# Expert layer on one Trainium2 core: 76 instead of 72 of 128 expert columns by fetched rows

## The chip, the cores and the metric

One core of a Trainium2 chip. The metric is device time in microseconds for one execution of the whole program (both transformer blocks); less is better. Engines are named as in the profile: PE (matrix engine), PEld (its weight loads), DVE (vector), ACT (scalar), POOL (GpSimd), SP (the queue that issues plain DMAs). POOL issues the indirect DMAs.

## What is computed

256 tokens of width 2048 pass a first block (two attentions, then an expert layer) and a second block (gated linear attention, pooling, an MLP of width 8192). The change touches the expert layer alone. Cut to what matters:

```python
q = (xt @ w_q).reshape(T, 8, 2, 128)                  # T = 256 tokens, 8 heads
s = einsum('thpd,hpnd->thpn', q, sub_keys)            # 128 keys in each half
# top 16 of each half, then top 16 of their 256 sums, per head
idx = i_first * 128 + i_second                        # one of 16384 experts
g = softmax(top_s)                                    # 8 x 16 = 128 experts a token
a = einsum('td,ted->te', xt, expert_u[idx])
y = einsum('te,ted->td', g * gelu(a), expert_v[idx])
```

So each token uses 128 of 16384 experts. With the experts as a grid of 128 x 128, the second half of the index is called the column here.

## The kernel before

Nearly all products are made to full precision by splitting both sides into a high and a low part (`hi_lo`, L196: ACT makes the high part, DVE the low one) and adding three matmuls (`mm3`, L217). `stream` (L204) loads a 512 KB piece of a weight into a buffer `r` and splits it into `h` and `l`; three buffers of each are in turn. PE's work is almost all on line L192, the helper `mm`.

The expert layer (`experts`, L903) computes a = x·u for **all** 16384 experts, one grid column a step (i = 0 to 127, 48 matmuls of 256 columns and two 512 KB loads of `u` a step). What follows depends on the column:

- **Columns below PICKED** (72): the activations go, four columns at a time (`lot`, 512 KB), to a table `picked` in DRAM. Of these columns only the experts that tokens have chosen are used: `pack` (L1113) sorts each group of 32 tokens' choices into 21 packs (PACKS) of 128 slots. The choices fill a group's packs from the first on, so that the last of the 21 are partly or wholly empty. For each of the 8 x 21 = 168 packs `fetch_act` (L1152) gathers the 128 activations and `fetch_row` (L1156) gathers up to 128 rows of 8 KB from `v_rows`; an empty slot points beyond the table and moves nothing. `multiply` (L1163) adds a pack's rows, weighted, into the group's output with four matmuls of 512 columns, which the profile counts as eight.
- **Columns from PICKED on** (GRID = 56): the activations stay in SBUF in `gridt` (56 columns x 256 tokens), multiplied by the gates, which `build` (L1080) and `apply` (L1094) spread over the grid with one-hot matmuls, four tokens at a time (64 times). Then `dense_rows` (L862) multiplies the whole grid with these columns of `v`: two halves of the output (d = 0, 1), one step a column, each step a 512 KB load of `v`, its split, the split of the column's weights, and 12 matmuls of 512 columns.

The steps run in this order: x·u for i = 0 to 127 (the u stage), then 2 x 56 steps of `dense_rows` (the v stage). Packing and building lie between the steps of the u stage, from i = 23 and i = 57 on. The picks (`picks`, L1177) are woven in by `unit` (L1228): each half step of the u stage from i = PICKED + LEADP = 75 on, and each v step up to the 40th of the second half (LASTY), adds PACE = 0.84 to a credit; at 3 (LOT) three packs are multiplied at once, back to back. After a pack's `multiply`, POOL issues the fetch of the pack six later (FETCH = 6 buffers) and the gather of activations twelve later. At i = PICKED - 1 the last `lot` is stored, twelve gathers of activations are issued, and DVE's `weigh` (L1160), which multiplies gates and activations four packs at a time, waits for them. When the grid's steps reach LASTY, the picks are done (16 steps remain); their sums are added to the result from DRAM (`add_y`, L1302). A branch behind it (`beyond`) works off what does not fit into 21 packs of a group; it runs only if a group has more than 21 x 128 = 2688 choices.

At the start of the v stage SP also loads 2 MB of the saved residual (`h2t<-h_keep`). `gridt` serves as scratch for the choosing of experts before the grid is filled; `carve` cuts tables from its end, one of them `pk`, a constant of 260 floats a partition.

Of the kernel before, what the change touches and what calls it, by code (L numbers as in the profile page):

```python
# [10 lines left out]
F32 = mybir.dt.float32  # L11
# [15 lines left out]
T = 256  # L27
NM = 16
TM = T + NM
PICKED = 72  # L30
GRID = 128 - PICKED
GROUP = 32
PACKS = 21
# [58 lines left out]
def _layout(a):  # L92
# [34 lines left out]
    v = a["peer_v"][0].reshape(128, 128, D)  # L127
    L["v"] = v[:, PICKED:].reshape(128, GRID, 2, 1024).transpose(2, 1, 0, 3).reshape(2 * GRID, 128, 1024)
    L["v_rows"] = v[:, :PICKED].reshape(128 * PICKED, D)

# [175 lines left out]
def bc(ap, shape):  # L306
    return ap.to_broadcast(shape)
# [531 lines left out]
FIRST, RATE = 57, 4  # L839
FETCH = 6  # L840
AHEAD, SOON = 12, 4
LASTY = 40
LOT = 3
LEADP, PACE = 3, 0.84


def topk16(S, jobs):
# [14 lines left out]
def dense_rows(S, wp, src, nk, get, evac, last=0, last_pool=None):  # L862

    mm = S.mm
    for d in range(2):
        accs = [[S.bank() for _ in range(2)] for _ in range(2)]

        def products(i, t, w, v, cols=(0, 1)):  # L870
            ts = slice(t * 128, t * 128 + 128)
            for a, b, first, end in ((w[0], v[0], True, False), (w[0], v[1], False, False), (w[1], v[0], False, True)):
                for c in cols:
                    mm(accs[t][c], a[:, ts], b[:, c], start=first and i == 0, stop=end and i == nk - 1)

        kept = []
        for i in range(nk):
            hold = d == 1 and i >= nk - last
            v = S.stream(src[d * nk + i], 2, 512, last_pool if hold else None)
            pool = last_pool if hold else wp  # L880
            w = [pool.tile([128, T], F32R, tag=f"w{x}", name=S.name("w")) for x in "hl"]
            S.hi_lo(get(i), *w)
            if hold:
                kept.append((i, w, v))
                products(i, 0, w, v)
            else:
                for t in range(2):
                    products(i, t, w, v)
            yield d, i
        yield d, nk  # L890
        for t in range(2):
            for c in range(2):
                if t == 1:
                    for i, w, v in kept:
                        products(i, 1, w, v, (c,))
                evac(d, t, c, accs[t][c])
# [6 lines left out]
def experts(S, I, x2, r2, started, keep, bst, grid, alloc_xn, close_x2, close_xn, late, picked, y_rows):  # L903
# [12 lines left out]
    def carve(*shape, dt=F32):  # L916
        n = int(np.prod(shape))
        end[0] -= n
        t = scratch[:, end[0]:end[0] + n].bitcast(dt)
        if len(shape) > 1:  # L920
            t = t.rearrange("p (a n) -> p a n", a=shape[0])
        if len(shape) > 2:
            t = t.rearrange("p a (b n) -> p a b n", b=shape[1])
        return t
# [13 lines left out]
    sc_ = carve(2, 16, 128)  # L938
    keysT = carve(16, 128)
    bcr = carve(T)  # L940
    pk = carve(260)
    spare = [carve(T) for _ in range(4)]
    S.load(keysT, I["keysT"])
    S.load(pk, I["c_pick"])

    def renorm(k):
# [34 lines left out]
    ow = ob.enter_context(tc.tile_pool(name="oneh", bufs=2))  # L981
# [15 lines left out]
    def choose():  # L997
        iota16 = S.iota[:, 0:16]
        for t in range(2):
# [57 lines left out]
            n = es[:, 0:1]  # L1057
            po.tensor_scalar(x, ii[:, 1], PICKED - 0.5, None, ALU.is_lt)
            ve.tensor_reduce(n, x, axis=AX, op=ALU.add)
            ve.tensor_scalar(y, S.ones, n, None, ALU.mult)  # L1060
            po.tensor_scalar(x, slots[:, 1, ts], PICKED - 0.5, None, ALU.is_lt)
            yield
# [17 lines left out]
    def build(t0):  # L1080

        iota = bc(S.iota[:, None, :], [128, 4, 128])
        of = lambda s, n: bc(slots[:, s, t0:t0 + 4][:, :, None], [128, 4, n])
        oh = ow.tile([128, 4, 128], F32R, tag="oh", name=S.name("oh"))
        ec = ow.tile([128, 4, GRID], F32, tag="ec", name=S.name("ec"))
        gv = ow.tile([128, 4, 2, GRID], F32R, tag="gv", bufs=1, name=S.name("gv"))
        ve.tensor_tensor(oh, iota, of(0, 128), op=ALU.is_equal)
        ve.tensor_tensor(ec, iota[:, :, PICKED:], of(1, GRID), op=ALU.is_equal)
        ve.tensor_tensor(gv[:, :, 1], ec, of(3, GRID), op=ALU.mult)
        for tt in range(4):  # L1090
            act.activation(gv[:, tt, 0], ec[:, tt], AF.Copy, scale=slots[:, 2, t0 + tt:t0 + tt + 1])
        made[t0] = oh, gv, ec
# [109 lines left out]
    def beyond():  # L1202

        more = 4096 // 128 - PACKS
        for g in range(8):
            for _ in pack(g, PACKS, more, 0):
                pass
            out = S.bank()
            for n in range(more):
                fetch_act(n)  # L1210
                fetch_row(n, fetched[n % FETCH])
                weigh(n)
                multiply(out, n, fetched[n % FETCH], n == 0, n == more - 1)
            stage = rw.tile([128, 512], F32, tag="stage", name=S.name("stage"))
            for c in range(4):
                S.load(stage[GROUP * c:GROUP * c + GROUP], y_rows[GROUP * g:GROUP * g + GROUP, 512 * c:512 * c + 512])
            ve.tensor_tensor(stage, stage, out, op=ALU.add)
            for c in range(4):
                S.load(y_rows[GROUP * g:GROUP * g + GROUP, 512 * c:512 * c + 512], stage[GROUP * c:GROUP * c + GROUP])
# [8 lines left out]
    def unit():  # L1228

        nonlocal credit  # L1230
        credit += PACE
        if credit >= LOT:
            for _ in range(LOT):
                next(side, None)
            credit -= LOT

    for i in range(128):
# [29 lines left out]
        if i == FIRST - 2:  # L1267
            for _ in bg:
                pass
            S.token = None  # L1270
            for f in fetched + [got]:
                po.memset(f, 0.0)
            for n in range(FETCH):
                fetch_row(n, fetched[n])
            build(0)
            ahead = 4
# [25 lines left out]
    def add_y(h, t, c):  # L1302
        y = rw.tile([128, 4, T], F32, tag="lot", name=S.name("y")).rearrange("p a b -> p (a b)")
        cs = slice(1024 * c, 1024 * c + 1024)
        po.dma_start(y, y_rows[t * 128:t * 128 + 128, cs])
        ve.tensor_tensor(h[:, t, cs], h[:, t, cs], y, op=ALU.add)
# [5 lines left out]
    for d, i in dense_rows(S, wp, I["v"], GRID, lambda i: grid[:, i], evac):  # L1312
        if d == 0 and i < GRID or d == 1 and i < LASTY:
            unit()
        if d == 1 and i == LASTY:
            for _ in side:
                pass
            S.pe_token = None
        if d == 1 and i == LASTY:
            n = nc.values_load(most_i[0:1, 0:1], min_val=0, max_val=4096)  # L1320
            with tc.If(n > 128 * PACKS):
                beyond()
        if d == 1 and LASTY < i <= LASTY + 2:
            add_y(h, i - LASTY - 1, 0)
        step(d, i)
# [356 lines left out]
    mst.close()  # L1682


FEAT = 47


class Plan:
# [20 lines left out]

    def alloc_x2(self):  # L1710
        self.bst = ExitStack()
        self.grid = self.bst.enter_context(self.S.tc.tile_pool(name="grid", bufs=1)).tile([128, GRID, T], F32, name="gridt")
        return self.parts("x2", side="left", first=192)

    def late(self):
# [11 lines left out]
        def step(d, i):  # L1727
            if d == 0:
                return
            if i == 0:  # L1730
# [4 lines left out]
                self.close("meta")  # L1735
            if i in (FEAT, FEAT + 6):
                self.features((i - FEAT) // 6)
            if i == GRID:
# [19 lines left out]
def program(tc, I, out):  # L1758
    with ExitStack() as st:
        S = Core(tc, st)  # L1760
        dram = st.enter_context(tc.tile_pool(name="dram", bufs=1, space=DRAM))
        keep = dram.tile([2, 128, D], F32, name="h_keep")
        base = S.const.tile([128, 384], F32, name="base")
        S.ident, S.iota, S.ones = base[:, 0:128], base[:, 128:256], base[:, 256:384]
        S.gains = S.const.tile([128, 98], F32, name="gains")
        S.load(S.gains, I["gains"])
        S.load_base = lambda: S.load(base, I["c_base"])
        warm = S.const.tile([128, 1], F32, name="warm")
        S.nc.vector.memset(warm, 0.0)
        S.nc.scalar.copy(warm, warm)  # L1770
        R = Plan(S, I)
        x2, r2, started = front(S, I, keep, R.alloc_x2, lambda j, x2: query(S, I, j, x2))
        picked = dram.tile([128, PICKED, T], F32, name="picked")
        y_rows = dram.tile([T, D], F32, name="y_rows")
        h = experts(S, I, x2, r2, started, keep, R.bst, R.grid, lambda: R.parts("xn"), lambda: R.close("x2"), lambda: R.close("xn"), R.late,
                    picked, y_rows)
        R.rest()
        back(S, I, h, R.u, R.started, R.ssn, lambda: R.close("ub", "ua"), out)
        R.close("h2")
# [11 lines left out]
```

## Time and profile before

| what | value |
|---|---|
| median of 3 runs (lowest to highest) | 2735.54 us (2732.2 to 2744.61) |
| the profiled execution | 2743.11 us |
| its span (first to last instruction) | 2741.0 us |
| PE busy | 2668.8 us, 97% |
| DVE, ACT, POOL busy | 62%, 49%, 25% |
| mean granted PE clock | 0.992 |
| u stage, first 72 steps | 425 to 855 us |
| u stage, 56 steps with grid and picks | 855 to 1292 us |
| v stage, steps with picks | 1292 to 1640 us |

"DMA share" is the busy share of the core's 16 DMA engines, added up over packets, so it can show slightly over 1. Busy time of PE is made of modelled ends: matmuls overlap, and the distance between starts says more than the duration of one. An idle time stands in brackets before what ended it.

### The profile page before, as it was taken

The page shows a single profiled execution, that of the slowest core. Times are in us where ns is not written, and L with a number is a line of the kernel's source. Part 1 is how long each engine was busy: PE and PEld are TensorE (multiplying, and loading weights), DVE is VectorE, ACT ScalarE, POOL GpSimd, SP SyncE. Part 2 cuts the span into 40 slices and gives each one's busy share as a digit, 9 for nine tenths or more (in the row PEclk, how much of TensorE's full clock was granted, in tenths as well). Part 3 has the DMA queues.
Part 4 walks back from the last instruction along what each step waited for, and adds up shares of the span by engine and source line. Part 5 has one row for each costly group of instructions (what it writes and reads, how often), then busy time and mean ns, then how long its engine had stood idle before and what let it go on. Part 6 is the DMA issues. An engine that isn't in the chain of part 4 may idle for free. (4 is left out here: it accounts for less than half of the span.)

```text
span 2741.0 us, 48520 instructions
## 1 busy us (share of the span) xinstructions
PE 2668.8 (97%) x18644; PEld 2328.6 (85%) x18644; DVE 1710.7 (62%) x3048; ACT 1336.7 (49%) x2330; POOL 683.8 (25%) x764
## 2 busy tenths in 40 slices
PE   7999999999999999999999997999999999999998
PEld 6977899999998888887666666998889999988886
DVE  5867787768866676774455455645554444566665
ACT  5655544434354444443444444534455555555554
POOL 1300003244613656665564520102000000000000
PEclk9999999999999999999999998999999999999999
DMA  6533756676665888899999985454666666666665
GB/s 214 156 121 107 224 174 195 207 249 222 189 196 162 323 329 328 319 365 354 373 391 374 363 308 187 135 152 137 187 186 195 196 193 193 194 195 194 189 196 162
DMA packets 161727, 625.89 MB, mean 228 GB/s; under 512 B 25849, under 2 KB 26873, under 8 KB 141321
## 3 DMA queue, kind: packets, MB, share of 16 engines
q1 hardware_dynamic: 131344, 462.77, 52.2%
q0 software_dynamic: 30144, 159.95, 14.9%
q8 instruction: 148, 2.42, 0.3%
q14 instruction: 91, 0.75, 0.1%
HBM read 625.33 MB, written 15.73 MB: 234 GB/s over the span
## 5 line engine op out<-in xcount | busy, mean ns | idle before, releaser
L198 DVE TENSOR_TENSOR l<-r,h 128x1024 fp32r<-128x1024 f32 (+3 forms) x838 | 1027.4, 1228 | 618.1 <-ACT h L197 592.5
L197 ACT ACTIVATE h<-r 128x1024 fp32r<-128x1024 f32 (+3 forms) x838 | 878.2, 1049 | 922.8 <-PE bank L192 656.0
L192 PE MATMUL bank<-xnh,l 128*128 128x256 f32 x2048 | 575.1, 281 | 11.7 <-DVE l L198 6.2
L192 PE MATMUL bank<-xnh,h 128*128 128x256 f32 x2048 | 582.4, 284 | 3.5 <-ACT h L197 2.7
L192 PE MATMUL bank<-xnl,h 128*128 128x256 f32 x2048 | 573.9, 280 | 0.6 <-issue 0.5
L192 PE MATMUL bank<-h,w 128*128 128x512 f32 x1920 | 523.5, 391 | 3.6 <-ACT w L197 2.0
L192 PEld LDWEIGHTS bank<-h,w 128*128 128x128 f32 x1920 | 357.6, 188 | 102.1 <-issue 18.4
L192 PEld LDWEIGHTS bank<-xnh,h 128*128 128x128 f32 x2048 | 391.7, 191 | 15.9 <-issue 7.1
L192 PEld LDWEIGHTS bank<-xnh,l 128*128 128x128 f32 x2048 | 388.0, 189 | 14.6 <-DVE l L198 7.2
L192 PEld LDWEIGHTS bank<-xnl,h 128*128 128x128 f32 x2048 | 388.4, 190 | 0.9 <-issue 0.8
L192 PE MATMUL bank<-l,w 128*128 128x512 f32 x960 | 297.4, 390 | 0.9 <-DVE l L198 0.9
L192 PE MATMUL bank<-zh,h 128*128 128x256 f32 x1024 | 283.0, 276 | 0.0
L192 PE MATMUL bank<-zl,h 128*128 128x256 f32 x1024 | 282.9, 276 | 0.0
L192 PE MATMUL bank<-zh,l 128*128 128x256 f32 x1024 | 282.9, 276 | 0.0
L1148 POOL DMA_INDIRECT fetched<-v_rows,at_row x168 | 205.5, 1223 | 230.4 <-PE bank L192 197.2
L192 PEld LDWEIGHTS bank<-l,w 128*128 128x128 f32 x960 | 179.9, 188 | 39.8 <-DVE l L198 2.2
L1148 POOL DMA_INDIRECT got<-picked,at_act x168 | 193.7, 1153 | 56.4 <-issue 49.7
L192 PEld LDWEIGHTS bank<-zh,l 128*128 128x128 f32 x1024 | 192.3, 188 | 0.0
L192 PEld LDWEIGHTS bank<-zh,h 128*128 128x128 f32 x1024 | 192.2, 188 | 0.0
L192 PEld LDWEIGHTS bank<-zl,h 128*128 128x128 f32 x1024 | 192.2, 188 | 0.0
L1124 POOL TENSOR_TENSOR what<-mine,facts 128x126 bf16<-128x126 f32 x256 | 140.2, 577 | 173.7 <-PE bank L1127 156.8
L1668 POOL TENSOR_TENSOR h2t<-h2t,fw 128x512 f32<-128x512 f32 x4 | 6.4, 1642 | 638.7 <-ACT jk L1666 638.7
(452 smaller groups left out, 3921.8 us busy)
## 6 DMA issues: line engine op xcount, KB each, us to landing
r<-u SPq DMA_DIRECT2D x256, 512.0 KB
r<-w SPq DMA_DIRECT2D x256, 512.0 KB
r<-v SPq DMA_DIRECT2D x112, 512.0 KB
r<-w_out SPq DMA_DIRECT2D x64, 512.0 KB
r<-wq SPq DMA_DIRECT2D x32, 512.0 KB
r<-w_in_c SPq DMA_DIRECT2D x24, 384.0 KB
picked<-lot SPq DMA_DIRECT2D x18, 512.0 KB
r<-w_v SPq DMA_DIRECT2D x16, 512.0 KB
```

What stands on the lines that cost most here:

```text
L192: i = self.nc.tensor.matmul(*args, **kw)
L197: self.nc.scalar.activation(hi, src, AF.Copy)
L198: self.order(self.nc.vector.tensor_tensor(lo, src, hi.bitcast(F32), op=ALU.subtract))
L1124: po.tensor_tensor(what[:, tt], bc(mine[:, tt][:, None, :], [128, 6, n]), bc(facts[:, :, t0 + tt][:, :, None], [128, 6, n]), op=ALU.mult)
L1148: i = po.indirect_dma_start(*args, **kw)
L1668: po.tensor_tensor(hs, hs, fw[:, cs_], op=ALU.mult)
```

## The change

PICKED goes from 72 to 76, so GRID from 56 to 52. LASTY and FEAT (a step of the v stage at which the next block's first work begins) are now written from GRID, and lie as far from the end of the v stage as before (16 and 9 steps). PACE goes from 0.84 to 0.91. The scratch tables no longer fit into the smaller grid, so `pk` gets a place of its own beside it. PACKS stays at 21. The layout of `v` and `v_rows` follows PICKED.

```diff
-PICKED = 72
+PICKED = 76
 GRID = 128 - PICKED
 GROUP = 32
 PACKS = 21
...
-LASTY = 40
+LASTY = GRID - 16
 LOT = 3
-LEADP, PACE = 3, 0.84
+LEADP, PACE = 3, 0.91
...
     bcr = carve(T)
-    pk = carve(260)
     spare = [carve(T) for _ in range(4)]
     S.load(keysT, I["keysT"])
+    pk = S.pk[:, :260]
     S.load(pk, I["c_pick"])
...
-        ec = ow.tile([128, 4, GRID], F32, tag="ec", name=S.name("ec"))
+        ec = ow.tile([128, 4, 56], F32, tag="ec", name=S.name("ec"))[:, :, :GRID]
...
-FEAT = 47
+FEAT = GRID - 9
...
-        self.grid = self.bst.enter_context(self.S.tc.tile_pool(name="grid", bufs=1)).tile([128, GRID, T], F32, name="gridt")
+        p = self.bst.enter_context(self.S.tc.tile_pool(name="grid", bufs=1))
+        self.grid = p.tile([128, GRID, T], F32, name="gridt")
+        self.S.pk = p.tile([128, 320], F32, name="pk")
```

Where instructions move, at two places. **DVE in the v stage**, from the last pack of a lot of three (L1166 makes a pack's weights `w` from slot and gate) to the first of the next lot; a row `w<-gridt` is one step of the grid. Before:

```order
L1166 TENSOR_SCALAR w_17582<-base,tok,gate 128x32
L198 TENSOR_TENSOR w_17418<-gridt,w_17417 128x256
L198 TENSOR_TENSOR l_17435<-r_17433,h_17434 128x1024
L1161 TENSOR_TENSOR gate<-gate,got 128x4
L198 TENSOR_TENSOR w_17440<-gridt,w_17439 128x256
L198 TENSOR_TENSOR l_17493<-r_17491,h_17492 128x1024
L198 TENSOR_TENSOR w_17498<-gridt,w_17497 128x256
L198 TENSOR_TENSOR l_17515<-r_17513,h_17514 128x1024
L198 TENSOR_TENSOR w_17520<-gridt,w_17519 128x256
L1166 TENSOR_SCALAR w_17682<-base,tok,gate 128x32
```

and now:

```order
L1166 TENSOR_SCALAR w_17620<-base,tok,gate 128x32
L198 TENSOR_TENSOR w_17455<-gridt,w_17454 128x256
L198 TENSOR_TENSOR l_17509<-r_17507,h_17508 128x1024
L198 TENSOR_TENSOR w_17514<-gridt,w_17513 128x256
L198 TENSOR_TENSOR l_17531<-r_17529,h_17530 128x1024
L1161 TENSOR_TENSOR gate<-gate,got 128x4
L198 TENSOR_TENSOR w_17536<-gridt,w_17535 128x256
L1166 TENSOR_SCALAR w_17698<-base,tok,gate 128x32
```

Between two lots stand four steps in the first piece and three in the second. Both kinds occur in both kernels: in PE's order of the v stage 27 lots stand there before and now, 15 of them with four and 11 with three steps ahead before, 8 with four and 18 with three now (the first lot has fewer).

**DVE where the picks start**, from the last one-hot table before the first `weigh` (L1161) on. Before:

```order
L1087 TENSOR_TENSOR oh_10485<-base,slots 128x512
L1161 TENSOR_TENSOR gate<-gate,got 128x4
L1260 TENSOR_TENSOR gridt<-gridt,gelu_10383 128x64
L198 TENSOR_TENSOR l_10508<-r_10506,h_10507 128x1024
L1106 TENSOR_TENSOR ec_10305<-ec_10305,bank_10396 128x4
```

and now:

```order
L1087 TENSOR_TENSOR oh_10830<-base,slots 128x512
L1260 TENSOR_TENSOR gridt<-gridt,gelu_10729 128x80
L1161 TENSOR_TENSOR gate<-gate,got 128x4
L198 TENSOR_TENSOR l_10853<-r_10851,h_10852 128x1024
L1106 TENSOR_TENSOR ec_10651<-ec_10651,bank_10742 128x4
```

The first `weigh` stands four steps later in the u stage (the grid's first column then has 80 gated tokens in place of 64), and the low part `l` of a piece of `u` still stands behind it.

## Rows read from the trace of the kernel before

**Rows 1.** The page's part 2, DMA in 40 slices of the span.

```profile
DMA  6533756676665888899999985454666666666665
```

**Rows 2.** Busy time by stretch: stretch, length, each engine's busy time, clock, DMA.

```profile
core 0: us, PE busy (x) PEld busy (x) DVE busy (x) ACT busy (x) POOL busy (x), PEclk, DMA share, GB/s
...
855.00:895.00 40.00, 33.32 (x264) 31.55 (x267) 24.03 (x58) 16.88 (x44) 17.25 (x20) 0.91 0.41 130
895.00:1292.00 397.00, 392.00 (x3398) 327.65 (x3391) 272.09 (x585) 186.54 (x467) 252.26 (x253) 1.00 0.90 337
1292.00:1340.00 48.00, 45.04 (x233) 28.86 (x235) 20.73 (x38) 17.48 (x27) 23.09 (x21) 1.00 1.02 401
1340.00:1600.00 260.00, 259.16 (x1370) 176.14 (x1363) 133.35 (x225) 106.90 (x150) 145.67 (x122) 1.00 0.97 374
1380.00:1420.00 40.00, 40.00 (x212) 27.22 (x209) 20.10 (x36) 15.81 (x23) 22.75 (x20) 1.00 1.02 410
```

**Rows 3.** Groups of instructions by line, whole span: busy, mean ns, idle before.

```profile
L198 DVE TENSOR_TENSOR l<-r,h 128x1024 fp32r<-128x1024 f32 (+3 forms) x838 | 1027.4, 1228 | 618.1 <-ACT h L197 592.5 <-issue 23.5
L192 PE MATMUL bank<-fetched,w 128*32 128x512 f32 x1344 | 155.8, 596 | 0.0
L198 DVE TENSOR_TENSOR w<-gridt,w 128x256 fp32r<-128x256 f32 x112 | 47.2, 422 | 40.3 <-PE bank L192 34.1 <-issue 5.6 <-ACT w L197 0.2
L1099 PE MATMUL bank<-gv,oh 128*128 128x112 f32 x256 | 39.2, 274 | 3.5 <-DVE ec L1106 2.5 <-DVE tmp L1134 0.4 <-DVE gv L1089 0.3
```

**Rows 4.** PE's timeline in the v stage, lots of three packs: start, duration.

```profile
1297.88 2.78 PE L192 MATMUL bank<-fetched,w 128*32 128x512 f32 x24
...
1309.73 2.78 PE L192 MATMUL bank<-fetched,w 128*32 128x512 f32 x24
...
1327.14 2.78 PE L192 MATMUL bank<-fetched,w 128*32 128x512 f32 x24
...
1338.81 2.78 PE L192 MATMUL bank<-fetched,w 128*32 128x512 f32 x24
...
1366.46 2.78 PE L192 MATMUL bank<-fetched,w 128*32 128x512 f32 x24
...
1377.58 2.78 PE L192 MATMUL bank<-fetched,w 128*32 128x512 f32 x24
...
1391.41 2.78 PE L192 MATMUL bank<-fetched,w 128*32 128x512 f32 x24
...
1491.29 2.78 PE L192 MATMUL bank<-fetched,w 128*32 128x512 f32 x24
...
1506.35 2.78 PE L192 MATMUL bank<-fetched,w 128*32 128x512 f32 x24
```

**Rows 5.** Waits from 1292 to 1640 us: who for whom, total, times, longest.

```profile
POOL fetched L1148 <- PE bank L192: 100.4, 28, 7.1
ACT h L197 <- DMA r<-v: 85.6, 46, 4.4
...
PEld bank L192 <- DMA fetched<-v_rows,at_row: 5.2, 15, 0.4
```

**Rows 6.** The page's part 3, the queue of POOL's indirect DMAs: packets, MB, share.

```profile
q0 software_dynamic: 30144, 159.95, 14.9%
```

**Rows 7.** DMA from 1340 to 1600 us in 40 slices of 6.5 us.

```profile
GB/s 408 273 272 398 363 370 425 410 407 407 409 416 390 410 291 233 320 401 309 409 411 409 390 410 411 402 352 382 376 204 374 394 316 413 417 386 363 414 405 402
```

**Rows 8.** Timeline where the picks start: PE's and DVE's longest idle times.

```profile
866.71 0.38 PE L192 MATMUL bank<-xnh,l 128*128 128x256 f32 x1 [1.07 <-issue]
...
872.84 0.39 PE L192 MATMUL bank<-xnh,l 128*128 128x256 f32 x1 [3.12 <-issue]
...
865.17 0.16 DVE L1161 TENSOR_TENSOR gate<-gate,got 128x4 f32<-128x4 f32 x1 [5.01 <-DMA got<-picked,at_act]
...
871.08 0.16 DVE L1161 TENSOR_TENSOR gate<-gate,got 128x4 f32<-128x4 f32 x1 [3.25 <-DMA got<-picked,at_act]
...
876.85 0.16 DVE L1161 TENSOR_TENSOR gate<-gate,got 128x4 f32<-128x4 f32 x1 [3.64 <-DMA got<-picked,at_act]
```

## The prediction

> **What bounds the kernel now.** I began with the table of the profile: PE is busy 97% of the span, the next engine 62%. So the span is PE's work plus PE's gaps, and a change is worth what it takes from either. The DMA row comes next [rows 1], because the change trades loads of one kind for loads of another: it shows 8 and 9 tenths only from slice 14 to 23, which is where picks run, and 4 to 6 afterwards. The reader is to see that the DMA engines are a second candidate there, and only there.
>
> By stretch [rows 2]: from 895 to 1292 us (u stage with picks) PE is busy 392 of 397 us at a DMA share of 0.90; from 1340 to 1600 us (v stage with picks) 259.16 of 260 us at 0.97 and 374 GB/s. The two limits lie on top of each other in the v stage, and PE is still the one that ends last: within that stretch the best 40 us moved 410 GB/s with PE busy 40.00 of 40. Only at the start of the v stage, where 2 MB of residual come on top, does PE lose 3 us of 48, at 401 GB/s and share 1.02. In slices of 6.5 us the rate stands at 405 to 417 for several slices in a row and hardly goes above (425 once) [rows 7]. I read 410 GB/s as what the DMA engines can give here.
>
> PE's own timeline gives the prices [rows 4]. Between lots of three packs lie three or four grid steps: 1366.46 to 1377.58 is 11.12 us with three steps, 1377.58 to 1391.41 is 13.83 us with four. One grid step (12 matmuls) is therefore **2.71 us**, and a lot 11.12 - 3 x 2.71 = 2.99 us. These are distances between starts, so they need no busy times. Longer intervals show PE's losses: 1297.88 to 1309.73 (three steps) is 0.73 us too long, 1309.73 to 1327.14 (four) 3.58, 1327.14 to 1338.81 (three) 0.55, and 1491.29 to 1506.35 (four; the halves of the output change there) 1.23. Together 6.1 us in the whole v stage.
>
> **The change, part by part.**
>
> *Eight grid steps go* (4 columns, two halves): 8 x 2.71 = **-21.7 us** on PE, the bound. With each go a 512 KB load, a split of it and a split of the column's weights, on DVE 1.23 + 0.42 us [rows 3]; DVE, ACT and SP are not the bound, so this counts nothing by itself.
>
> *The picks stay 168*, 56 lots of 2.99 us, 29 in the u stage and 27 in the v stage before and after. The busy time of their matmuls is 155.8 us [rows 3] in both. 0 us. They do stand closer: 27 lots over 87 steps in place of 95 (the order pieces above).
>
> *The one-hot matmuls* (L1099) shrink from 112 to 104 columns. They take 39.2 us [rows 3]; by columns they would save 39.2 x 8/112 = 2.8 us, and nothing if their weight loads set the pace. I take -1, nearer to nothing, since 0.15 us for one is already longer than its few columns need beside the 512-column matmuls at 2.71/12 = 0.23 us.
>
> *Four columns go to the table instead of the grid*: one more store of 512 KB (1.3 us of DMA time at 410 GB/s, at a place where nothing is full) and four DVE multiplications fewer. 0, between 0 and +1.3.
>
> *The picks start four steps later.* There DVE waits three times for gathered activations (5.01, 3.25 and 3.64 us), PE runs dry behind it (1.07 and 3.12 us, [rows 8]), and the clock falls: 0.91 of full over 40 us [rows 2], so 40 x 0.09 = 3.6 us lost to it. In the new order the same three waits stand with the same splits of `u` behind them. 0; if a split fell behind one wait more, +3 to +5, and as much the other way.
>
> *The bytes.* This is what can take the gain back. The queue of indirect DMAs moved 159.95 MB [rows 6], 2.1 MB of it `y` for the result, the rest 8 KB rows: some 19,260. Counted from the inputs it is 19,255 of 32,768 choices below column 72, and 20,186 below column 76: 931 rows or 7.6 MB more, against 8 x 0.524 = 4.2 MB less of `v`. A pack carries 0.984 MB on the mean in place of 0.939. The fullest group of 32 tokens has 2596 choices and 21 packs hold 2688, so the branch for overflow stays shut.
>
> For the v stage with picks, before: 96 x 0.524 + 81 x 0.939 + 2.1 (residual) + 1 (sums stored) = 129.5 MB; PE needs 96 x 2.71 + 27 x 2.99 = 341 us, and with the 6.1 us of losses it took 347, that is 373 GB/s, as the row says. After: 88 x 0.524 + 81 x 0.984 + 3.1 = 129.0 MB, while PE needs only 88 x 2.71 + 80.7 = **319 us**. For no loss at all the DMA engines would have to give 404 GB/s throughout. At 410 they need 315 us, so PE still ends last; but with 1% to spare every crowding costs. Already now ACT waits 46 times for a load of `v`, 85.6 us in all, and PE pays 15 small waits for rows [rows 5]; the other side of it, POOL waiting 100.4 us for PE to free a buffer, is the slack that is left. Lower bound of the loss: the 6.1 us of before, so +0. Upper bound: if 374 GB/s, the mean over 260 us, were all there is, 129.0/0.374 = 345 us, so +20 over before's losses. I take a rate of 390, between the two but nearer to what 40 us showed without harm: 331 us, a loss of 12, **+5.7 us** against before.
>
> *In the u stage* a step with picks needs 2 x 0.524 + 1.82 x 0.984 = 2.84 MB in place of 1.05 + 1.68 x 0.939 = 2.63. At (1292 - 855)/56 = 7.8 us a step that is 364 instead of 337 GB/s, below 410, but the last steps are faster and join the crowd. PE lost 5 us of 397 there; I add **+1.5 us**, between 0 and 5.
>
> Sum: -21.7 - 1 + 5.7 + 1.5 = **-15.5 us**. The profiled execution took 2743.1 us, 7.6 above the median of the runs; from the median of 2735.5 this gives **2720 us**.
>
> **The rivals.**
>
> *A. All of the gain.* The fetches have six buffers, a group's last packs are nearly empty and let the queue catch up, and the crowd costs no more than before: -21.7 - 1 = -23, 2712 us. For it: 410 GB/s with PE at 40.00 of 40 [rows 2]. Against: at 401 GB/s beside the residual's load PE did lose 3 us.
>
> *B. The DMA engines are the bound.* If what long stretches show, 374 GB/s, is the limit, the v stage takes 345 us in place of 347, and the sum is -2 - 1 + 1.5: 2734 us, no change. For it: share 0.97 and ACT's waits for `v`. Against: [rows 7], slice after slice near 410. The Trainium skill ("DMA: Bandwidth & Descriptors", Where 436 GB/s comes from) says that transfers between HBM and SBUF are bound at about 358 GB/s by the memory's share of a core. By that limit the v stage would take 129.0/0.358 = 360 us (an estimate from that page), 13 us longer than now; the trace, with 374 over 260 us, disagrees.
>
> *C. Rows come late lot by lot, and the kernel is slower.* A group's first 19 or 20 packs are full, 1.05 MB each; an interval of three steps then asks 3 x 0.524 + 3 x 1.05 = 4.72 MB in 11.12 us, 424 GB/s, above anything sustained. Most of the intervals are now of that kind. If the buffers did not even this out and the rate were 374, such an interval would last 12.6 us, 1.5 late, and 27 lots would lose 40 us: -21.7 + 40 = +18, 2754 us. It decides from 0.8 us a lot. Against: before the change an interval of three steps with full packs asked for 424 just the same, and the three intervals of that length in [rows 4] lost 0.73, 0.55 and 0 us, two of them beside the residual's load.
>
> *D. The start of the picks gets worse*, by one more wait of DVE and one more fall of the clock: +5 + 4, 2729 us.
>
> **How the numbers follow.** About 0.5%, 13.7 us, is what a measurement of this kernel can tell from no change. Forecast (losses of 3 to 10 us more than before): 0.48; A: 0.20; B: 0.18; D: 0.07; C: 0.07. Of the forecast's 0.48 about a third (losses over 8 us) stays within 0.5%. So faster 0.20 + 0.32 = 0.52; within 0.16 + 0.18 + 0.07 = 0.41; slower 0.07. The forecast's own range is 2715 to 2726; the range that holds 8 of 10 reaches from A's 2709 (the whole 2.8 us of the one-hot matmuls with it) to B and D with a few us of scatter, 2739, and leaves out C.
>
> **What would show it.** PE's timeline of the v stage: intervals of 11.1 and 13.8 us between lots as before, 18 of three steps, with more of them 0.5 to 1 us too long; the stage with picks about 331 us long. DMA there at a share of 1.0 and 385 to 400 GB/s. ACT's wait for `v` well over 85.6 us, POOL's for PE below 100. Software queue at 167.5 MB. If the stage lasts 319 to 325 us, A was right; if the rate stays near 374 and PE shows gaps in every interval, B or C. The prediction would be wrong altogether if the time moved outside these two stages, where nothing was touched.

## The result and the profile after

**2722.0 us** (median of 4 runs, 2721.1 to 2728.1) against 2733.9 us (4 runs of the kernel before beside them, 2731.0 to 2744.6): ratio 0.995, 95% interval 0.9935 to 0.9965. The profiled execution took 2728.1 us, its span 2726.3 us: 14.7 us less than the span of before.

The page's parts 1, 2 and 3 for the kernel after, the engines' busy time, the slices of the span and the queues (packets, MB, share):

```profile
PE 2647.0 (97%) x18548; PEld 2310.3 (85%) x18548; DVE 1691.5 (62%) x3020; ACT 1322.4 (49%) x2306; POOL 677.9 (25%) x764
...
DMA  6533756676566689989999985444666666666665
...
q0 software_dynamic: 30144, 167.57, 15.5%
```

The software queue moved 7.6 MB more than before [rows 6]. The tenths of the DMA row rise at slices 13, 16 and 17 and fall at 11, 14, 18 and 27 [rows 1].

Busy time by stretch for the kernel after (columns as in [rows 2]); the 5 us stretches cut out the place discussed next:

```profile
895.00:1290.00 395.00, 389.32 (x3327) 324.75 (x3328) 263.70 (x580) 178.49 (x451) 252.91 (x257) 0.99 0.91 346
1290.00:1340.00 50.00, 42.59 (x216) 27.22 (x219) 22.22 (x40) 19.31 (x28) 21.36 (x21) 0.93 0.98 382
1340.00:1600.00 260.00, 255.42 (x1358) 170.27 (x1351) 128.49 (x223) 101.79 (x142) 146.93 (x125) 1.00 0.99 391
...
1305.00:1310.00 5.00, 0.00 (x0) 0.00 (x0) 0.27 (x2) 1.76 (x3) 2.60 (x3) 0.97 1.02 412
1310.00:1315.00 5.00, 3.91 (x9) 3.14 (x10) 3.97 (x5) 0.76 (x2) 0.00 (x0) 0.50 0.92 319
```

The long stretch of the v stage went from 374 to 391 GB/s [rows 2]. But PE lost more per microsecond in the 50 us ahead of it: 7.4 of 50 us idle there, 4.6 of 260 behind (3.0 of 48 and 0.8 of 260 before).

PE's timeline of the kernel after, lots of three packs in the v stage (start, duration):

```profile
1291.74 2.78 PE L192 MATMUL bank<-fetched,w 128*32 128x512 f32 x24
...
1315.65 3.18 PE L192 MATMUL bank<-fetched,w 128*32 128x512 f32 x24
...
1385.43 2.78 PE L192 MATMUL bank<-fetched,w 128*32 128x512 f32 x24
...
1401.08 2.78 PE L192 MATMUL bank<-fetched,w 128*32 128x512 f32 x24
...
1509.08 2.78 PE L192 MATMUL bank<-fetched,w 128*32 128x512 f32 x24
...
1522.91 2.78 PE L192 MATMUL bank<-fetched,w 128*32 128x512 f32 x24
...
1534.03 2.78 PE L192 MATMUL bank<-fetched,w 128*32 128x512 f32 x24
```

1509.08 to 1522.91 is 13.83 us (four steps) and 1522.91 to 1534.03 is 11.12 (three): the prices of [rows 4] hold to 0.01 us. One interval is far off: 1291.74 to 1315.65 is 23.91 us, **10.1 too long**. 1385.43 to 1401.08 is 1.8 too long; three more, from 1473.2, 1484.9 and 1545.1, lose 0.6, 1.9 and 1.8. Against the prices of [rows 4] (a four-step interval 13.83, three 11.12) the stage lost 16.5 us, 6.1 before.

So the time went like this (the starts of the first matmul of the v stage and of its last lot are read from PE's timeline):

| from | to | before | after | difference |
|---|---|---|---|---|
| start of span | first matmul of the v stage | 1292.3 | 1288.9 | -3.4 |
| that | last lot | 341.5 | 330.2 | -11.3 |
| that | end of span | 1107.2 | 1107.2 | 0.0 |

1.0 us of the -3.4 lies ahead of the expert layer, where nothing was touched. The v stage's -11.3 is -21.7 for eight steps and **+10.4** for the losses.

What fills the long interval, in the timelines of PE, DVE and POOL of the kernel after (start, duration, in brackets idle time before and what ended it):

```profile
1301.18 0.73 PE L192 MATMUL bank<-h,w 128*128 128x512 f32 x2 [0.98 <-ACT w L197]
...
1303.59 1.07 PE L192 MATMUL bank<-h,w 128*128 128x512 f32 x4
1311.09 1.22 PE L192 MATMUL bank<-l,w 128*128 128x512 f32 x2 [6.43 <-DVE l L198]
1312.11 1.91 PE L192 MATMUL bank<-h,w 128*128 128x512 f32 x4
...
1309.73 0.16 DVE L1161 TENSOR_TENSOR gate<-gate,got 128x4 f32<-128x4 f32 x1 [8.10 <-DMA got<-picked,at_act]
1309.81 1.22 DVE L198 TENSOR_TENSOR l<-r,h 128x1024 fp32r<-128x1024 f32 x1
...
1299.78 0.62 POOL L1724 TENSOR_TENSOR mT<-mT,gains 128x256 f32<-128x256 f32 x1 [9.44 <-PE bank L192]
1300.67 1.03 POOL L1148 DMA_INDIRECT fetched<-v_rows,at_row  x1 [0.28 <-issue]
1302.01 1.00 POOL L1148 DMA_INDIRECT got<-picked,at_act  x1 [0.30 <-issue]
1303.32 1.00 POOL L1148 DMA_INDIRECT fetched<-v_rows,at_row  x1 [0.31 <-issue]
1304.62 0.99 POOL L1148 DMA_INDIRECT got<-picked,at_act  x1 [0.30 <-issue]
1305.92 1.00 POOL L1148 DMA_INDIRECT fetched<-v_rows,at_row  x1 [0.30 <-issue]
1307.22 1.00 POOL L1148 DMA_INDIRECT got<-picked,at_act  x1 [0.30 <-issue]
```

SP's issue of `mT`'s load in the kernel after, and below it POOL's row for `mT` in the kernel before:

```profile
1291.35 0.38 SPq L182 DMA_DIRECT2D mT<-metaT  x1
...
1302.65 0.62 POOL L1722 TENSOR_TENSOR mT<-mT,gains 128x256 f32<-128x256 f32 x1 [8.05 <-DMA mT<-metaT]
```

To be read from the bottom up. POOL is held for 9.4 us by a step for the second block, `mT`. It waits for its own load: SP issues the load at 1291.35 us and it lands 8.3 us later, just before `mT` starts. (The row of the kernel after names PE, since a signal of PE came at the same moment; the row of the kernel before names the load.) Then POOL issues three row fetches of up to 1 MB and three small gathers in turn. DVE reaches `weigh` at 1301.6, and it waits 8.10 us for its gathered activations; the last gather for its packs (96 to 99) is the first of these three, issued at 1302.01 us, 7.7 us before `weigh` starts. The split `l` of a piece of `v` is queued right behind it, so PE stands idle for 6.43 us, while the DMA engines are busy throughout (share 1.02, 412 GB/s). Then PE runs at 1.2 GHz (granted clock 0.50 from 1310 to 1315 us; a matmul row of four takes 1.91 us in place of 1.07). 0.98 + 6.43 us idle and some 2.7 at the half clock are the 10.1.

The waits from 1292 to 1640 us in the kernel after (who for whom, total, times, longest):

```profile
POOL fetched L1148 <- PE bank L192: 96.6, 28, 9.4
ACT h L197 <- DMA r<-v: 86.5, 48, 5.1
...
DVE gate L1161 <- DMA got<-picked,at_act: 53.5, 16, 8.1
...
PEld bank L192 <- DMA fetched<-v_rows,at_row: 4.8, 14, 0.4
```

ACT's waits for `v` and PE's for rows are as before [rows 5]. DVE's wait for gathers, which my prediction did not follow into this stage, went up to 53.5 us; in the kernel before it was:

```profile
DVE gate L1161 <- DMA got<-picked,at_act: 36.5, 14, 5.5
```

### The profile page after: what moved, and what is told of

Read it like the earlier page. It is cut to its first block, busy times and chain, and to the rows that moved or that the text cites. A ratio compares the mean times of both kernels' runs of the same rounds, so it can differ in the third digit from the quotient of the medians.

```text
span 2726.3 us, 48218 instructions
## 1 busy us (share of the span) xinstructions
PE 2647.0 (97%) x18548; PEld 2310.3 (85%) x18548; DVE 1691.5 (62%) x3020; ACT 1322.4 (49%) x2306; POOL 677.9 (25%) x764
## 3 DMA queue, kind: packets, MB, share of 16 engines
q0 software_dynamic: 30144, 167.57, 15.5%
## 5 line engine op out<-in xcount | busy, mean ns | idle before, releaser
L192 PE MATMUL bank<-h,w 128*128 128x512 f32 x1856 | 507.2, 392 | 6.2 <-DVE w L198 3.6
L192 PEld LDWEIGHTS bank<-h,w 128*128 128x128 f32 x1856 | 346.4, 188 | 102.7 <-issue 17.6
L192 PE MATMUL bank<-l,w 128*128 128x512 f32 x928 | 288.1, 391 | 6.5 <-DVE l L198 6.4
```

Source lines behind the costliest of these rows:

```text
L192: i = self.nc.tensor.matmul(*args, **kw)
```

## The experiments

Two theories are set against each other: **bytes** (the DMA engines' rate sets the loss, as the prediction argued) and **the order** of the instructions on DVE and POOL. From kernel 6 on the second reads **the gathers**: a gather lies behind whole row fetches, and what DVE has queued behind `weigh` waits with it. Each batch has its own runs of the kernel before; batches are 1 to 4, 5 to 8, 9 to 11, and 12. "Losses" are all that the v stage's intervals took over the prices above.

**1 and 2. Half of the rows, at 72 and at 76 columns.**

```diff
-              bounds_check=128 * PICKED - 1, oob_is_err=False)
+              bounds_check=64 * PICKED - 1, oob_is_err=False)
```

> The kernel before with the rows' limit halved: a slot whose expert lies in the lower half of the grid's rows moves nothing, so about half of the fetched rows are left out (and so is their part of the result); every instruction and its order stay. Theory (crowded DMA engines cause the gaps of the v stage): the 6.1 us of gaps there vanish, intervals of 11.1 and 13.8 us throughout, and some of the 5 us of the u stage; 2724 us or 10 less than before. Rival (the gaps come from the order on DVE and PE, not from bytes): the gaps stay, 2734 us.

> The changed kernel with the same half of the fetched rows left out. Theory: its 16.6 us of gaps in the v stage vanish too, so 2722 - 17 = 2705 us, less a little in the u stage, and the distance to the kernel before with half the rows is the bare price of eight grid steps and narrower one-hot matmuls, -21.7 to -24.5 us. Rival (the order): the long gap at the start of the v stage stays at 10 us, 2722 us, and the distance stays near 12 us.

Measured: 2731.1 us at 72 columns (ratio 0.9938 [0.9914, 0.9962]) and 2715.3 at 76 (0.9891 [0.9873, 0.9908]). Busy time by stretch at 72 and DVE's waits from 895 to 1640 us in it:

```profile
1340.00:1600.00 260.00, 260.00 (x1381) 176.88 (x1379) 138.99 (x228) 110.93 (x151) 142.63 (x120) 1.00 0.80 269
...
DVE gate L1161 <- DMA got<-picked,at_act: 35.3, 19, 5.0
```

At 76:

```profile
1340.00:1600.00 260.00, 260.00 (x1391) 174.64 (x1389) 136.78 (x226) 107.61 (x147) 142.39 (x121) 1.00 0.82 277
...
DVE gate L1161 <- DMA got<-picked,at_act: 39.2, 19, 5.7
```

With 269 and 277 GB/s PE has not one gap in 260 us. Losses are 0 at 72 and 3.6 us at 76, all of these at the start of the stage, where a wait of 5.7 us for gathers is left. The medians are 15.8 us apart, less than the 21.7 to 24.5 expected. From the stage's first matmul to its last lot it is 335.3 and 317.2 us: 18.1 apart, 21.7 without the losses. So eight steps are worth what the forecast said, and the rows' traffic does trigger the losses. By which way the two runs don't tell: DVE's wait fell with the bytes, from 85.9 us in the kernel before to 35.3.

**3. Closer picks alone**, at 72 columns.

```diff
-LEADP, PACE = 3, 0.84
+LEADP, PACE = 3, 0.91
```

> The kernel before with PACE 0.91 alone: 72 columns, 112 grid steps, the picks closer together and done some 16 half steps earlier. Theory (what was given back is the price of closer picks): PE's work is the same, the stretch with picks loses 5 to 10 us more to gaps, 2739 to 2744 us. Rival (the closeness costs nothing, the gaps came from the larger packs or from where the picks start): 2734 us, within 2 us.

Measured: 2754.0 us, ratio 1.0038 [1.0023, 1.0052], 9.4 us slower. The profile has the price in two places. From the first matmul of the u stage to the first of the v stage it is 888.8 us, with three lots (9.0 us) more than before in it; without them that is 4.4 us longer than the 875.4 before. The v stage lost 10.2 us to gaps, 4.0 more than before. At the end of the u stage stand two long waits in `weigh`, and in the v stage one interval, at 1315 us, is 7.9 us too long:

```profile
1271.05 0.16 DVE L1161 TENSOR_TENSOR gate<-gate,got 128x4 f32<-128x4 f32 x1 [7.06 <-DMA got<-picked,at_act]
...
1285.94 0.16 DVE L1161 TENSOR_TENSOR gate<-gate,got 128x4 f32<-128x4 f32 x1 [8.81 <-DMA got<-picked,at_act]
...
1326.15 1.06 ACT L197 ACTIVATE h<-r 128x1024 fp32r<-128x1024 f32 x1 [10.96 <-DMA r<-v]
...
1327.86 1.22 PE L192 MATMUL bank<-h,w 128*128 128x512 f32 x2 [4.28 <-ACT w L197]
```

No `weigh` stands in that interval's stop: ACT waits 10.96 us for a load of `v`, and PE 4.28 us behind it. So there are two ways to run dry at the start of the v stage, a late gather and a late load of `v`. In the v stage closeness without fewer bytes of `v` costs 4.0 us, less than half of the change's extra losses.

**4. The residual's 2 MB in eight pieces**, meant to spread over the stage.

```diff
-    for t in range(2):
-        S.load(h[:, t], keep[t])
+    def residual(c, t):
+        cs = slice(512 * c, 512 * c + 512)
+        S.load(h[:, t, cs], keep[t][:, cs])
...
+        for c in range(2):
+            for t in range(2):
+                if d == 0 and i == 12 + 10 * (2 * c + t):
+                    residual(c, t)
+                if d == 1 and i == LASTY + 2 + 2 * (2 * c + t):
+                    residual(2 + c, t)
```

> The changed kernel with the 2 MB of residual not loaded at the start of the v stage: one half in four pieces over steps 12 to 42 of the first output half, the other after the picks are done. Theory (the load at the start is what starves PE there): the long interval of 21.2 us shrinks to 11 to 13 us and the fall of the clock behind it goes, 8 to 11 us less, 2711 to 2714 us. Rival (the whole stretch is short of DMA rate, and the wait only moves): 1 MB less in the stretch is worth 2.5 us, 2719 us, with gaps elsewhere.

Measured: 2731.8 us, 0.9943 [0.9926, 0.996]; the long interval is there, 23.5 us, 9.6 too long, with a `weigh` that waits 7.4 us up to 1318.7. But the edit did not do what it was meant to. SP's timeline of this kernel:

```profile
1301.79 0.42 SPq L182 DMA_DIRECT2D h2t<-h_keep  x1
...
1304.56 1.88 SPq L182 DMA_DIRECT2D h2t<-h_keep  x2
...
1307.94 0.44 SPq L182 DMA_DIRECT2D h2t<-h_keep  x1
...
1320.46 0.42 SPq L182 DMA_DIRECT2D h2t<-h_keep  x1
...
1321.92 1.37 SPq L182 DMA_DIRECT2D h2t<-h_keep  x3
```

Eight loads written up to 84 steps apart were issued within 22 us: the order of issue pulled them to the front. Four, 1 MB, lie ahead of the long wait, four behind it. So the run says only that the interval stays the same with half of the residual; that the residual has no part in it is not shown.

**5 to 8. The change once more, `mT` early, gathers further ahead, and both.** In 6, `mT` is loaded and multiplied in a place of its own before the experts, and in the v stage only copied, on ACT:

```diff
-        S.load(self.mT, I["metaT"])
-        S.nc.gpsimd.tensor_tensor(self.mT, self.mT, bc(S.gains[:, G_N12:G_N12 + KD][:, :, None], [128, KD, NM]), op=ALU.mult)
+        S.nc.scalar.copy(self.mT, self.mT0)
```

In 7 it is one number, and 8 has both edits:

```diff
-AHEAD, SOON = 12, 4
+AHEAD, SOON = 20, 4
```

> The changed kernel once more, unaltered, beside the three below on one chip. Every theory expects about 0.995 of the kernel before, and in the profile the long interval at the start of the v stage (21.2 + 2.7 us where 13.8 are needed) with a fall of the clock behind it. If that interval is 14 to 16 us here, it is scatter of a run and not a property of the order.

> The changed kernel with one small thing taken out of POOL's queue: the product mT (the second block's meta tokens by their gains), which stands between two fetches at the start of the v stage and waits for its own load, is made early in a spare place and only copied on ACT later. Theory P (POOL's queue stands still behind mT for 9.4 us, rows and activations are asked for late, DVE's weigh waits 8.1 us, PE runs dry): the start interval falls to 14 to 16 us and the clock stays, 7 to 10 us less than the changed kernel, 0.9915 to 0.9925 of before. Theory D (the DMA engines are simply full there): the interval stays at 20 us or more, 0.995.

> The changed kernel with the activations gathered 20 packs ahead instead of 12 (AHEAD), so that weigh finds them landed. Theory W (PE starves because DVE, waiting in weigh for a gather that stands in the queue behind whole rows, holds back the splits behind it): DVE's wait for gathers from 895 to 1640 us falls from 118.6 us to under 30, most of the 16.5 us of gaps in the v stage go, also those of 1.8 us later on; 10 to 14 us less, 0.990 to 0.9915 of before. Theory P: only part of it, since the rows themselves are still asked for late; the start interval 16 to 20 us. Theory D: no gain, the gaps move to PE's wait for rows.

> Both edits in the changed kernel. Theories P and W together: gaps of the v stage under 4 us in all, 12 to 15 us less than the changed kernel, 0.9895 to 0.991 of before, with the DMA engines at 395 GB/s or more from 1340 to 1590 us. Theory D: the rate cannot rise over the 391 GB/s seen, and at least 8 us of gaps stay.

| kernel | us | ratio and interval | losses in the v stage | longest interval over its price |
|---|---|---|---|---|
| 5, the change | 2726.1 | 0.9937 [0.9916, 0.9959] | 13.7 | 9.7 |
| 6, `mT` early | 2727.1 | 0.9937 [0.9914, 0.9959] | 12.2 | 6.6 |
| 7, gathers 20 ahead | 2733.7 | 0.9968 [0.9955, 0.998] | 15.3 | 10.6 |
| 8, both | 2730.4 | 0.9958 [0.9944, 0.9971] | 13.1 | 7.2 |

The long interval is no accident of one execution. `mT` makes about 3 us of it, half of which comes back as a loss of 1.5 us in the interval behind. In 6 and 8 `weigh` still waits 7.5 and 8.3 us there, and right behind it ACT waits 10.6 and 10.8 us for a load of `v`. Gathers further ahead, which I expected to end the wait, did not, and kernel 7 is slower than kernel 5: its fastest execution (2731.0 us) is behind the slowest of kernel 5 (2730.4). Where the picks start it issues 20 gathers in a row, and PE has one stop more there, of 5.01 us at 914.0 us. DVE's and POOL's timelines of kernel 7 show why the wait stays:

```profile
1320.27 0.16 DVE L1161 TENSOR_TENSOR gate<-gate,got 128x4 f32<-128x4 f32 x1 [8.03 <-DMA got<-picked,at_act]
...
1311.29 1.03 POOL L1148 DMA_INDIRECT fetched<-v_rows,at_row  x1 [0.28 <-issue]
1312.62 0.99 POOL L1148 DMA_INDIRECT got<-picked,at_act  x1 [0.30 <-issue]
```

This `weigh` is for packs 104 to 107, while PE has done 90; its last gather was issued at 1312.62 us and it waits until 1320.27, though PE needs the gates only some 50 us later. The order of issue puts `weigh` as soon behind its gathers as their issue allows: with gathers eight packs earlier, `weigh` stands eight packs earlier too, and blocks what is behind it just as long. DVE waited 95.5 us in all, 103.3 in kernel 5 beside it.

**9 and 11. `weigh` kept in its place**, at 76 and, with the same edit, at 72 columns. `weigh` and the packs' weights `w` get one token, which holds them in the order in which they are written, so `weigh` for a pack stays behind the `w` of the packs before it. Gathers run 20 ahead, reached by two a pack, so that the start still issues 12:

```diff
+    def stamp(i):
+        if S.pe_token:
+            tc.stamp_issue_order_token(i.ins, 'weigh')
...
-        ve.tensor_tensor(gate[:, n:n + m], gate[:, n:n + m], got[:, n:n + m], op=ALU.mult)
+        stamp(ve.tensor_tensor(gate[:, n:n + m], gate[:, n:n + m], got[:, n:n + m], op=ALU.mult))
...
-            if n + AHEAD < NP:
-                fetch_act(n + AHEAD)
+            for _ in range(2):
+                if asked < min(NP, n + AHEAD + 1):
+                    fetch_act(asked)
+                    asked += 1
```

> The changed kernel with the gathers 20 packs ahead (grown from 12 over the first picks) and, new, weigh kept in its place on DVE among the packs' weights; with the gathers ahead alone the order had pulled each weigh forward to 7 to 10 us behind its own gather, so that it waited as before. Theory W: DVE's wait for gathers from 895 to 1640 us falls from 100 us and more to under 25; the long interval at the start of the v stage falls from 23.5 to 15 to 18 us and its fall of the clock goes, the later gaps of 1.5 to 2 us go; 0.989 to 0.991 of before. Theory D (DMA engines full, whatever DVE does): DVE's wait goes, but ACT and PE wait for rows and for v in its place; gaps of the v stage stay at 10 us or more, 0.9935 to 0.995.

> The kernel before with the same cure (weigh in place, gathers 20 ahead). Its gaps in the v stage were 6.1 us, so Theory W expects 3 to 8 us less than before, 0.997 to 0.999; and the distance to the same cure at 76 columns should come near the bare price of eight grid steps, 20 to 24 us. Theory D: 1.000, and a distance of 12 to 15 us.

Measured at 76: 2721.6 us, 0.9918 [0.9895, 0.9941]. Busy time by stretch, and waits from 895 to 1640 us:

```profile
1290.00:1340.00 50.00, 47.34 (x280) 32.48 (x276) 20.91 (x41) 18.46 (x28) 29.14 (x26) 1.00 1.02 402
1340.00:1580.00 240.00, 239.77 (x1281) 160.50 (x1273) 122.77 (x214) 95.04 (x136) 131.23 (x113) 1.00 1.01 405
...
ACT h L197 <- DMA r<-v: 133.4, 68, 4.6
...
DVE gate L1165 <- DMA got<-picked,at_act: 3.8, 1, 3.8
```

The ratio's interval reaches from one theory's forecast to the other's; the profile decides between them. The same bytes, in less time, at a share of 1.01 and **405 GB/s over 240 us**, with PE busy 239.77 of 240. DVE's wait fell from 103.3 us in kernel 5 to 3.8, the losses from 13.7 us to 4.0, and the clock stays at 2.4 GHz in the whole v stage. ACT waits 133.4 us for `v` (99.6 in kernel 5), and PE's losses are the smallest of all kernels with 76 columns and all of the rows. From the first matmul of the stage to the last lot it is 317.6 us, against 330.2 for the change as it was.

The gain is the v stage's alone. Of the 103.3 us of waits in kernel 5, 49.7 lay in the u stage; they are gone but for 3.8, and the u stage takes 880.9 us in place of 878.8. There the waits cost PE nothing that shows. The longest stop that is left, 2.34 us of PE at 1323.7 us, stands behind ACT, which waits 3.08 us for a piece of `v` and then does a step for the second block ahead of the `w` that PE needs:

```profile
1321.38 1.89 ACT L1743 ACTIVATE mt<-mt 16x2048 f32<-16x2048 f32 x1
```

Measured at 72: 2739.8 us, 0.9988 [0.9972, 1.0003], hardly an effect:

```profile
1340.00:1580.00 240.00, 240.00 (x1269) 163.68 (x1268) 125.43 (x210) 100.24 (x138) 125.76 (x109) 1.00 0.96 374
```

Its losses are 4.6 us, 4.2 of them in one interval at 1304.7 (the same step on ACT, a stop of 2.29 us), and its stage lasts 339.9: the two cured kernels are 22.3 us apart there (21.7 without their losses), 18.2 by their medians. 374 GB/s, which the kernel before shows too, is what is asked for, not what can be given.

**10. The same with `mT` early. 12. The same with the residual's loads as in 4.**

> The same, and mT out of POOL's queue at the start of the v stage. Theories W and P: start interval 14 to 16 us, gaps of the v stage under 5 us in all, 0.988 to 0.990 of before. Theory D: the start interval stays over 19 us, as it did (20.5) with mT alone.

> The changed kernel with weigh kept in its place, gathers 20 ahead, and the 2 MB of residual spread as before (half of it after the picks). Theory W with the residual: what is left of gaps at the start of the v stage (2.6 us, and 7 in the run with mT out of the way) is the residual's load holding up v; it goes, gaps of the v stage under 2 us, 0.989 to 0.991 of the kernel before. Rival (the stage runs at the limit of the DMA engines, 405 GB/s at share 1.01, and any load put elsewhere in it shows up there): gaps of 3 us or more in the middle of the stage, 0.991 to 0.993.

Measured: 10: 2722.8 us, 0.9924 [0.9908, 0.9941], losses 7.1 in one interval, behind a wait of ACT for `v` of 10.1 us; the start did not get shorter than in 9. 12: 2717.3 us, 0.993 [0.9917, 0.9944], losses 10.3, of which 6.7 in one interval. In that interval ACT's timeline of kernel 12 has

```profile
1327.82 1.06 ACT L197 ACTIVATE h<-r 128x1024 fp32r<-128x1024 f32 x1 [9.79 <-DMA r<-v]
```

with the DMA engines full:

```profile
1325.00:1330.00 5.00, 0.76 (x2) 0.50 (x2) 1.09 (x1) 1.36 (x2) 2.29 (x3) 0.88 1.01 407
```

Between 1290 and 1330 us a load of `v` competes with nine row fetches and the residual, all eight pieces of which were issued between 1287.9 and 1305.9 us: again not spread. With `weigh` in its place, what is left at the start of the stage is a wait for `v`, as in kernel 3, with ACT's step for the second block behind it in 9 and 11; neither edit shows what makes the load late. That the rows held up behind `mT` and the residual together fill the DMA engines there is how I read the rows; it is not shown, since no run took the residual away.

**The fastest.** Kernels 9, 10 and 12 lie at 0.9918, 0.9924 and 0.993 of the kernel before, the change as it is at 0.995 and 0.9937. All three are faster than before, with the whole interval below 1; against the change their intervals overlap, no execution of the change stood beside them, and the 7 to 11 us by which their spans are shorter than those of the change's two profiles show only in part in the ratios. That `weigh` in its place makes the whole program faster than the change is therefore likely, and not shown.

Not tried: `weigh` in its place with gathers only 12 ahead, `pk` in its own place at 72 columns, and more than 76 columns.

## Why the prediction held, and where its working was wrong

The predicted 2720 us and its sum of -15.5 stand against a difference of 11.9 between the medians, 17.6 in the second batch (kernel 5), and 14.7 between the spans. By its own steps:

- **Eight grid steps, -21.7: right.** -21.7 between the two kernels with half the rows and between the two with `weigh` in its place, both without their losses, and intervals of 11.12 and 13.83 us to the hundredth.
- **One-hot matmuls, -1: right in kind.** The busy time of their group (L1099) went from 39.2 us [rows 3] to 38.6.
- **The crowding, +5.7: right sign, half the size, and the wrong mechanism.** It measured +10.4 (+7.5 in kernel 5). The step that failed is "I take a rate of 390": I put the rate between the mean of a long stretch (374 GB/s) and the best of a short one (410), below the 404 that PE asked for, and let the loss follow from bytes over rate. The rate is 405 when PE asks for it (kernel 9), so the limit of 374, on which rival B stands, falls as well. The Trainium skill ("DMA: Bandwidth & Descriptors", Where 436 GB/s comes from) gives about 358 GB/s for such transfers; 405 over 240 us disagrees. The 391 GB/s of the profile after, so near to the 390, was a consequence of PE's stops. The rows' bytes do trigger the losses (kernels 1 and 2), but by single transfers that come late, not by a mean rate. What was overlooked stands in [rows 8]: DVE waiting 3 to 5 us in `weigh` with a split behind it and PE dry. I took this for a matter of the start of the picks, though it goes on through both stages (85.9 us from 895 us on in the kernel before, 118.6 in the one after). At the start of the v stage, where the share is 1.02, a late load of `v` remains in kernels 9 to 12, and there the limit of the DMA engines may still be the cause; that stays open.
- **The u stage, +1.5: not settled.** From the first matmul of the u stage to the first of the v stage it is 875.4 us before, 873.0 after and 878.8 in kernel 5; two profiles of the same kernel differ by 5.8 us, more than the term.
- **The start of the picks, 0: right.** DVE waits 4.84, 2.95 and 3.79 us there (before: [rows 8]), and the clock is at half for as long as before (6.8 us in two pieces, from 896.7 us on and, before, from 874.0 us on).
- **The signs that were named.** Stage 331 us: no. The forecast counts 88 steps and 27 lots, 347 us before, and by that count the stage after takes 319 + 16.5 = 336 us; the 330.2 of the table above ends at the start of the last lot (341.5 before), and agrees with 331 by accident. 18 intervals of three steps, and a rate of 385 to 400 GB/s: 18, and 391. Queue 167.5 MB: 167.57. POOL's wait below 100: 96.6. ACT's wait for `v` "well over 85.6": it is 86.5 (96.1 in kernel 5), wrong, and a hint, since with the DMA engines as the limit it should have grown. "More intervals 0.5 to 1 us too long": no, one of 10 and four of 0.6 to 1.9.
- **The rivals.** A's stage of 319 to 325 us came only with `weigh` in its place: 319 + 4.0 = 323 by the forecast's count. C's price would show in every interval; most show 0.00. D did not occur. That closer picks alone cost 9.4 us (kernel 3) is what remains of C: it's a real cost, paid in a few places and not lot by lot.
- **A reading.** The DMA row of the kernel before shows 8 and 9 tenths in slices 14 to 24, not 23 [rows 1]; nothing rests on it.

So the number came out well partly by luck. The forecast has -16.0 us in the v stage and +0.5 ahead of it (-1 and +1.5). Measured are -11.3 and -3.4: two errors of opposite sign, and for the -3.4, which is within what two profiles of one kernel differ by, no run shows a cause. And 390 stood for one way of losing time where another acts, of nearly the same size.

## What to carry to other kernels

A wait of an engine costs what is queued behind it, if the engine that bounds the kernel needs that next (the same waits in the u stage cost nothing that shows). So when a change crowds a queue, look up each small transfer in that queue, who waits for it, and what stands behind the one that waits; the bandwidth comes second. A mean rate of a stretch is a demand unless something is late in it; one longer stretch at a share of 1.0 without a gap says more. And fetching earlier helps only if the use stays where it was: look whether the order of issue has moved it along.

## What was not expected of the hardware

- The 16 DMA engines gave 405 GB/s for 240 us, with 8 KB rows by the software queue and 512 KB loads mixed, and the matrix engine stood idle for 0.23 us of it.
- A gather of 128 x 4 bytes took 7.7 us from issue to use (1312.62 to 1320.27 in kernel 7), with one row fetch issued 1.3 us ahead of it in the same queue and two behind it. In kernel 6 it took 11.0 us (1301.43 to 1312.41).
- After an idle time of 6.43 us PE's granted clock was at half (1.2 GHz) for 6.8 us. After the idle times of 1.49 and 1.58 us in the same stage (1396.3 and 1493.8 us) it stayed at 2.4 GHz. The length of the idle time alone does not tell: after 2.29 us it fell in kernel 11 (0.52 from 1316 to 1319 us), after 2.34 us in kernel 9 (at 1323.7 us) it did not.
